# Three chunk splits on VectorE get a fixed place in its queue, in the feed-forward of one decoder layer

## The chip, the core and the metric

The kernel runs on one core of one Trainium2 chip. The metric is device time in microseconds (us) of one execution; lower is better. TensorE multiplies matrices and is called PE in the profile, VectorE is DVE, ScalarE is ACT, GpSimd is POOL, and SyncE, which only issues DMAs here, is SP. PEld is TensorE's weight load.

## What is computed

One layer of a decoder: a gated mix of two attention branches, an attention over 256 memory tokens, a feed-forward and a last normalisation, for 256 tokens of width 1024 in float32. The change lies in the feed-forward:

```python
hn = rmsnorm(h, norm_ffn_g[l])
gu = hn @ w_ffn_in[l]                       # (256, 1024) @ (1024, 2 * 2816)
h = h + (jax.nn.silu(gu[..., :FFN_HIDDEN]) * gu[..., FFN_HIDDEN:]) @ w_ffn_out[l]
...
return rmsnorm(h, final_norm_g)
```

## The kernel before

**Precision.** Every matrix is written as a high and a low part. The high part is a copy in TensorE's reduced float32 format, made by ScalarE; the low part is the source minus the high part, made by VectorE. That pair of operations is called a split. A product of two such matrices is three matmuls: high by high, high by low, low by high.

**Units.** The weights of the feed-forward come in chunks of 1 MB (128 by 2048 float32), one chunk for each unit of work. `FFN_PLAN` (line 90) lists 48 units, and TensorE works through them in this order, which is fixed by hand. The hidden width of 2816 is cut into 11 blocks of 256. Block 0 is made by two units of kind I (2 and 3). Blocks 1 to 10 are taken in pairs, and each pair by seven units of kind P, named P1 to P7: a scheme with seven products in place of eight, in which some products are of sums of token halves (`SS`) with sums of weight chunks, made earlier in DRAM. A unit of kind O multiplies one finished hidden block with its rows of `w_ffn_out` and adds to four accumulators `acc`. The units around the change are: 4 P6, 5 P7, 6 P5, 7 O of block 0, 8 P3, 9 P4 (all of the first pair), 10 P1 and 11 P2 of the second pair, 12 O of block 1, 13 P6, 14 P7, 15 P5, 16 O of block 2. A unit of kind P is 12 matmuls of 128 by 512, a unit of kind O is 24.

**Preparing a unit.** `prep_u(upto)` (line 1172) prepares units up to that number in the program's text: it fetches the chunk by a DMA from SP (line 1157, or 1164 for the chunk of a P2, tile `b`) and calls `halve` (line 1131), which makes the high part in two pieces on ScalarE (line 1146) and, for all but the first units, the low part in one piece on VectorE (line 1151). The fetched chunk lies in one of three buffers `raw`, or in a place that is free at that time (`rawx`). Units whose number divided by 4 leaves 1 put both parts into `px`, from unit 9 on; the others into three buffers `hi` and three `lo`. Behind the split of a P2 unit, GpSimd adds another chunk onto the fetched one by an accumulating DMA (line 1180), and P4 of the same pair uses that sum.

**Gates and turns.** When the products of a block and a token half are done, VectorE puts them together (`whole`, lines 1323 and 1325, tile `fc`), ScalarE takes the silu (`gate`, line 1240, tile `fg`), and VectorE multiplies (lines 1244 and 1246, tile `fu`). For unit 8 the gate reads the bank directly. `turn_hid(o)` (line 1248) then transposes block o on TensorE (line 1253, tile `hidT`) and splits it (lines 309 and 310, tile `hids`), so that a unit of kind O can use it. `TURNS` (line 95) says ahead of which unit a block is turned: block 0 ahead of unit 6, block 1 ahead of unit 10, block 2 ahead of unit 12.

**Order.** TensorE's instructions keep the order of the program's text. Those of the other engines and the DMA issues get an order when the program is built: a planner takes what its model of the chip finds ready, with the earlier one in the text first, and writes each engine's queue. On the chip each of these queues is then worked off in the written order, and an instruction whose operand isn't ready keeps those behind it waiting. Only units 5 and 6 are marked so that their splits keep the text's order.

The main loop (lines 1377 to 1390) runs over units 4 to 45: it prepares a unit some three or four ahead, turns a block where `TURNS` says so, and does the unit's matmuls.

Of the kernel before, what the change touches and what calls it, by code (L numbers as in the profile page):

```python
# [11 lines left out]
F32 = mybir.dt.float32  # L12
# [3 lines left out]
ALU = mybir.AluOpType  # L16
# [128 lines left out]
def build(tc, A, out):  # L145
    nc = tc.nc
    V, SC, G, PE, SY = nc.vector, nc.scalar, nc.gpsimd, nc.tensor, nc.sync
    with ExitStack() as ctx:
# [12 lines left out]
        def big(tag, name, shape=(128, 8, 256), dt=F32):  # L161
            return bp.tile(list(shape), dt, name=name, tag=tag)
# [103 lines left out]
        def by_k(w, k):  # L266
            return tuple(t.rearrange("p (k c) -> p k c", k=k) for t in w)
# [39 lines left out]
        def split(src, hi, lo, scale=None):  # L307
            if scale is None:
                SC.activation(hi, src, AF.Copy)
                V.tensor_tensor(lo, src, hi.bitcast(F32), op=ALU.subtract)  # L310
            else:
                SC.activation(hi, src, AF.Copy, scale=scale)
                V.scalar_tensor_tensor(lo, src, scale, hi.bitcast(F32), op0=ALU.mult, op1=ALU.subtract)
# [742 lines left out]
        def scores(x):  # L1056
            ps = bank("xs", (128, 2, 256))
            for t in range(2):
                a = slice(t * 128, (t + 1) * 128)
                for i in range(2):  # L1060
                    k = 2 * x + i
                    mm3t(ps[:, t], qxh[:, k, a], qxl[:, k, a], kxh[:, k], kxl[:, k], i == 0, i == 1)
            mx, s = small("xmx", [2]), small("xsum", [2])
            p = t2("xp", (128, 2, 256))
            for t in range(2):
                V.tensor_tensor_reduce(out=p[:, t], in0=ps[:, t], in1=mem["rows"], op0=ALU.mult, op1=ALU.max,
                                       scale=1.0, scalar=-3e38, accum_out=mx[:, t:t + 1])
            V.scalar_tensor_tensor(mx, mx, -1.0, one["r16"], op0=ALU.mult, op1=ALU.mult)
            for t in range(2):
                SC.activation(p[:, t], p[:, t], AF.Exp, scale=one["r16"][:, t:t + 1], bias=mx[:, t:t + 1],  # L1070
                              accum_out=s[:, t:t + 1])
            V.reciprocal(s, s)
            for t in range(2):
                V.tensor_scalar(p[:, t], p[:, t], s[:, t:t + 1], None, op0=ALU.mult)
            yield 1
            yield 1
            pT = bank("xT", (128, 2, 256))
            for m in range(2):
                for t in range(2):
                    PE.transpose(pT[:, m, t * 128:(t + 1) * 128], p[:, t, m * 128:(m + 1) * 128], ident)  # L1080
            split(pT, ph[:, x], pl[:, x])

        sg = []
        for c in range(4):
            gemm_f(H1, ev_sum(qxh, qxl, c))
            g = scores(c)
# [44 lines left out]
        def halve(raw, n):  # L1131
            def pin(z):
                if n in PINNED:
                    tc.keep_in_program_order(z)

            tags = PAIRS[n] if n < 6 else PAIRS[n % 4 + 2 if n % 4 == 1 else 0]
            if tags == "px":
                hi, lo = px[:, 0:2048], px[:, 2048:4096]
            elif tags:
                hi, lo = (big(tag, name, (128, 2048), F32R) for tag, name in zip(tags, ("hix", "lox")))  # L1140
            else:
                hi = wh.tile([128, 2048], F32R, name="hi", tag="hi")
                lo = wl.tile([128, 2048], F32R, name="lo", tag="lo")
            for c in range(2):
                a = slice(c * 1024, (c + 1) * 1024)
                pin(SC.activation(hi[:, a], raw[:, a], AF.Copy))  # L1146
            pieces = 2 if n < 2 else 1
            w = 2048 // pieces
            for c in range(pieces):
                a = slice(c * w, (c + 1) * w)  # L1150
                pin(V.tensor_tensor(lo[:, a], raw[:, a], hi[:, a].bitcast(F32), op=ALU.subtract))  # L1151
            return hi, lo

        def fetch(src):
# [6 lines left out]
        def operand(q, name):  # L1161
            if name == "P2" and q != DOUBLES[0]:
                blk[q] = big(next(homes), "b21", (128, 2048))
                tc.keep_in_program_order(SY.dma_start(blk[q], block(q, "21")))
                return blk[q]
            if name == "P4" and q in blk:
                return blk.pop(q)
            return fetch(scr[q][name] if name in scr[q] else block(q, {"P1": "11", "P2": "21", "P3": "22"}[name]))
# [3 lines left out]
        def prep_u(upto):  # L1172
            while made_u[0] <= min(upto, len(units) - 1):
                n = FIRST[made_u[0]] if made_u[0] < len(FIRST) else made_u[0]
                made_u[0] += 1
                u = units[n]
                raw = operand(u[1], u[2]) if u[0] == "P" else fetch(A["w"][where[u]])
                pair[n] = halve(raw, n)
                if u[0] == "P" and u[1] in blk and u[2] == "P2":
                    G.dma_start(raw, scr[u[1]]["P6"], accum_op=ALU.add)  # L1180
# [4 lines left out]
        ssq2 = cp.tile([128, 4], F32, name="ssq2")  # L1185
        v2 = cp.tile([128, 2], F32, name="v2")
        r2 = cp.tile([128, 2], F32, name="r2")
        h2g = {}

        def add_h2(t, c, ps):  # L1190
            d = H[:, t, c * 512:(c + 1) * 512]
# [27 lines left out]
        for t in range(2):  # L1219
            for c in range(2):  # L1220
                ps = mm.tile([128, 512], F32, name="pso", tag="mm")
# [12 lines left out]
        hid, acc, psi, hm = {}, {}, {}, {}  # L1234


        def gate(o, t, sign=1.0):
            ps = psi.pop((o, t))
            g = t2b("fg", (128, 256))
            SC.activation(g, ps[:, 0:256], AF.Silu, scale=sign)  # L1240
            if o not in hm:
                hm[o] = t2("fu", (128, 2, 256))
            if sign < 0:
                V.scalar_tensor_tensor(hm[o][:, t], ps[:, 256:512], sign, g, op0=ALU.mult, op1=ALU.mult)  # L1244
            else:
                V.tensor_tensor(hm[o][:, t], ps[:, 256:512], g, op=ALU.mult)

        def turn_hid(o):
            bk = mm.tile([128, 2, 256], F32, name="hidT", tag="mm")
            u = hm.pop(o)  # L1250
            for t in range(2):
                for j in range(2):
                    PE.transpose(bk[:, j, t * 128:(t + 1) * 128], u[:, t, j * 128:(j + 1) * 128], ident)
            z = o // 2 % 2
            if z not in hids:
                hids[z] = big(("B7", "B14")[z], "hids", (128, 2, 2, 2, 256), F32R)
            hd = hids[z][:, o % 2]
            split(bk, hd[:, 0], hd[:, 1])
            hid[o] = hd

        def out_part(o, w, t, c, home=None, u=0, v=512):
# [58 lines left out]
        def whole(q, t, ps, key):  # L1320
            c = t2("fc")
            if key == "4":
                V.scalar_tensor_tensor(c, ps, -1.0, kept.pop(key), op0=ALU.mult, op1=ALU.subtract)
            else:
                V.tensor_tensor(c, ps, kept.pop(key), op=ALU.add)
            psi[q, t] = c
            gate(q, t)

        def ffn_product(n):
            _, q, name = units[n]  # L1330
            w = by_k(pair[n], 4)
            key = {"P1": "A", "P6": "A", "P5": "A", "P3": "A", "P2": "B", "P7": "F", "P4": "F"}[name]
            first = name in ("P1", "P2", "P7")
            if first:
                bank_of[key] = mm.tile([128, 512], F32, name="pq" + key, tag="mm")
            ps = bank_of[key]
            product(ps, name, w, first)
            if name == "P1":
                keep("1", ps, t2("f1"))
            elif name == "P2":  # L1340
                whole(q + 1, 0, ps, "1")
            elif name == "P6":
                keep("2", ps, gf[:, 1024:1536])
            elif name == "P5":
                keep("4", ps, gf[:, 1536:2048])
                whole(q, 1, bank_of["F"], "4")
            elif name == "P3":
                psi[q, 0] = ps
                gate(q, 0, -1.0)
            elif name == "P4":  # L1350
                whole(q + 1, 1, ps, "2")

        def ffn_out(n):
            w = by_k(pair[n], 2)
# [20 lines left out]
            ffn_in(n, 1)  # L1375
        prep_u(7)
        for n in range(4, len(units) - 2):
            if n != 6:
                prep_u(max(n + 3, min(n + 4, 9)))
            for o in TURNS.get(n, ()):  # L1380
                turn_hid(o)
            prep_u(n + 3)
            u = units[n]
            if u[0] == "I":
                for t in range(2):
                    ffn_in(n, t)
            elif u[0] == "P":
                ffn_product(n)
            else:
                ffn_out(n)  # L1390
# [3 lines left out]
        n = NF // 2 - 1  # L1394
# [38 lines left out]
        with tc.manual_schedule(engines={E.Activation, E.DVE, E.Pool, E.SP}):  # L1433
# [24 lines left out]
            for i in range(2):  # L1458
                a = slice(512 + 256 * i, 768 + 256 * i)
# [46 lines left out]
```

## Time and profile before

| what | value |
|---|---|
| time, median of 3 runs | 612.86 us (612.53 to 612.93) |
| the profiled execution's own time | 612.86 us |
| its span, first to last instruction | 611.1 us |
| TensorE's mean granted clock | 0.998 of full speed |
| busy: TensorE, VectorE, ScalarE, GpSimd | 602.2, 448.9, 373.1, 110.0 us |
| feed-forward and end, in the span | from about 436 us |

A row of a timeline reads: start in us, duration in us, engine, line of the kernel, operation, the tile written and the tiles read, shape and type, and how many instructions were merged into the row; in square brackets, the time for which the engine sat idle before it and what ended that. A busy matmul row of 0.39 us overlaps the next one, as matmuls are pipelined. The chain that ended last follows the work back from the last instruction, each step to what released it.

### The profile page before, as it was taken

The page shows a single profiled execution, that of the slowest core. Times are in us where ns is not written, and L with a number is a line of the kernel's source. Part 1 is how long each engine was busy: PE and PEld are TensorE (multiplying, and loading weights), DVE is VectorE, ACT ScalarE, POOL GpSimd, SP SyncE. Part 2 cuts the span into 40 slices and gives each one's busy share as a digit, 9 for nine tenths or more (in the row PEclk, how much of TensorE's full clock was granted, in tenths as well). Part 3 has the DMA queues.
Part 4 walks back from the last instruction along what each step waited for, and adds up shares of the span by engine and source line. Part 5 has one row for each costly group of instructions (what it writes and reads, how often), then busy time and mean ns, then how long its engine had stood idle before and what let it go on. Part 6 is the DMA issues. An engine that isn't in the chain of part 4 may idle for free.

```text
span 611.1 us, 8304 instructions
## 1 busy us (share of the span) xinstructions
PE 602.2 (99%) x3093; PEld 502.9 (82%) x3093; DVE 448.9 (73%) x702; ACT 373.1 (61%) x603; POOL 110.0 (18%) x137
## 2 busy tenths in 40 slices
PE   8999999999999999999999999999999999999995
PEld 7888888888887887778888888888878888888884
DVE  7598867978756877658866566694896887878953
ACT  7695545333377676736447656684776667677732
POOL 3898100112200431000301403100000000000003
PEclk9999999999999999999999999999999999999999
DMA  8886688747995789957779778863949979796601
GB/s 346 348 305 197 217 252 327 246 139 285 322 257 220 242 260 285 330 203 317 275 216 308 233 280 225 253 215 132 351 158 335 369 267 391 235 383 220 248 2 69
DMA packets 21864, 156.79 MB, mean 257 GB/s; under 512 B 2752, under 2 KB 3392, under 8 KB 5312
## 3 DMA queue, kind: packets, MB, share of 16 engines
q1 hardware_dynamic: 18224, 134.46, 56.7%
q0 software_dynamic: 2880, 20.97, 17.4%
q10 hardware_dynamic: 720, 0.84, 0.4%
q8 instruction: 24, 0.39, 0.3%
q14 instruction: 16, 0.13, 0.1%
HBM read 155.21 MB, written 34.60 MB: 311 GB/s over the span
## 4 chain that ended last, share of the span: by engine, by line
PE 90%; DVE 5%; ACT 2%; issue 1%; POOL 0%; POOLq 0%; DVEq 0%; ACTq 0%
PE pst L262 13%; PE pst L264 13%; PE pst L263 13%; PE pqA L1311 8%; PE psf L283 7%; PE pqF L1311 4%; PE psf L284 4%; PE acc L264 3%; PE acc L263 3%; PE acc L262 3%; PE pqB L1311 2%; PE lp L637 2%; DVE lo L1151 1%; PE psg L538 1%; PE as L826 1%
## 5 line engine op out<-in xcount | busy, mean ns | idle before, releaser
L222 DVE TENSOR_TENSOR lo<-raw,hi 128x1024 fp32r<-128x1024 f32 (+1 forms) x128 | 156.5, 1233 | 56.5 <-ACT hi L221 56.1
L221 ACT ACTIVATE hi<-raw 128x1024 fp32r<-128x1024 f32 (+1 forms) x128 | 129.0, 1028 | 98.5 <-PE pst L264 79.3
L262 PE MATMUL pst<-hi,XX 128*128 128x512 f32 x224 | 90.4, 404 | 0.0
L264 PE MATMUL pst<-hi,XX 128*128 128x512 f32 x224 | 87.4, 390 | 0.0
L263 PE MATMUL pst<-lo,XX 128*128 128x512 f32 x224 | 87.3, 390 | 0.0
L264 PEld LDWEIGHTS pst<-hi,XX 128*128 128x128 f32 x224 | 42.0, 188 | 9.0
L262 PEld LDWEIGHTS pst<-hi,XX 128*128 128x128 f32 x224 | 42.1, 188 | 8.8 <-issue 0.7
L263 PEld LDWEIGHTS pst<-lo,XX 128*128 128x128 f32 x224 | 42.1, 188 | 7.9
L1151 DVE TENSOR_TENSOR lo<-raw,hi 128x2048 fp32r<-128x2048 f32 (+1 forms) x18 | 36.8, 2052 | 10.6 <-ACT hi L1146 10.5
L1146 ACT ACTIVATE hi<-raw 128x1024 fp32r<-128x1024 f32 x32 | 32.0, 1052 | 7.4 <-PE acc L264 5.3
L1151 DVE TENSOR_TENSOR lo<-rawx,hi 128x2048 fp32r<-128x2048 f32 x12 | 27.5, 2288 | 8.1 <-ACT hi L1146 8.1
L1146 ACT ACTIVATE hi<-rawx 128x1024 fp32r<-128x1024 f32 x24 | 24.1, 1051 | 5.9 <-PE acc L264 2.6
L1311 PE MATMUL pqA<-hi,SS 128*128 128x512 f32 x80 | 26.4, 390 | 0.0
L1180 POOL DMA_DIRECT2D b<-t x4 | 3.6, 894 | 124.3 <-DVE fu L1244 124.3
L264 PE MATMUL acc<-hi,hids 128*128 128x512 f32 x62 | 24.3, 392 | 0.7 <-DVE hids L310 0.7
L262 PE MATMUL acc<-hi,hids 128*128 128x512 f32 x62 | 24.4, 393 | 0.0
L263 PE MATMUL acc<-lo,hids 128*128 128x512 f32 x62 | 24.2, 390 | 0.0
L283 PE MATMUL psf<-H,hi 128*128 128x512 f32 x64 | 22.7, 398 | 0.0
L283 PE MATMUL psf<-M,hi 128*128 128x512 f32 x64 | 22.5, 394 | 0.0
L283 PE MATMUL psf<-XX,hi 128*128 128x512 f32 x64 | 22.4, 394 | 0.0
L743 POOL DMA_DIRECT2D t<-w x16 | 13.8, 878 | 46.7 <-DMA t<-w 32.1
L1151 DVE TENSOR_TENSOR lo<-b,hi 128x2048 fp32r<-128x2048 f32 x7 | 16.0, 2292 | 6.2 <-ACT hi L1146 6.2
(418 smaller groups left out, 1511.7 us busy)
## 6 DMA issues: line engine op xcount, KB each, us to landing
raw<-w SPq DMA_DIRECT2D x75, 1024.0 KB, 6.3
t<-w POOLq DMA_DIRECT2D x16, 1024.0 KB, 10.0
raw<-t SPq DMA_DIRECT2D x12, 1024.0 KB, 6.8
rawx<-w SPq DMA_DIRECT2D x10, 1024.0 KB, 7.2
rawx<-t SPq DMA_DIRECT2D x4, 1024.0 KB, 8.9
b<-w SPq DMA_DIRECT2D x4, 1024.0 KB, 9.3
b<-t POOLq DMA_DIRECT2D x4, 1024.0 KB, 8.5
raw<-w SPq DMA_DIRECT2D x4, 512.0 KB, 6.5
```

What stands on the lines that cost most here:

```text
L221: SC.activation(hi[:, a], raw[:, a], AF.Copy)
L222: V.tensor_tensor(lo[:, a], raw[:, a], hi[:, a].bitcast(F32), op=ALU.subtract)
L262: PE.matmul(ps, xh, h, start=first, stop=False)
L263: PE.matmul(ps, xh, l, start=False, stop=False)
L264: PE.matmul(ps, xl, h, start=False, stop=last)
L283: PE.matmul(ps, w[0][:, k, a], X2[:, :, k], start=k == 0, stop=False)
L284: PE.matmul(ps[:, 0], w[1][:, k, a], X2[:, 0, k], start=False, stop=k == 7)
L637: PE.matmul(ps[:, j], KS[:, a0 + j], QQ[:, a0 + j], start=True, stop=True)
L743: tc.keep_in_program_order(G.dma_start(t, block(q, name), accum_op=ALU.add, max_dma_last_dim=8192))
L1146: pin(SC.activation(hi[:, a], raw[:, a], AF.Copy))
L1151: pin(V.tensor_tensor(lo[:, a], raw[:, a], hi[:, a].bitcast(F32), op=ALU.subtract))
L1311: PE.matmul(ps, x[k], z[:, k], start=first and k == 0 and i == 0, stop=k == 3 and i == 2, skip_group_check=not first)
```

## The change

The program gives three low-part splits of `halve` an edge in VectorE's queue: the split of unit 9 is to come behind the low-part split of turn 0, that of unit 11 behind the gate's product of unit 8, and that of unit 13 behind both the gate's product of unit 9 and the low-part split of turn 1. Such an edge, `tc.issue_after(ins)`, is an order within one engine's queue; it adds no instruction and no semaphore. Since the edge can only name an instruction that is in the text already, the preparations move in the text: unit 9 is prepared after turn 0 (before: one unit earlier, ahead of the matmuls of unit 5), unit 11 after the matmuls of unit 8 (before: ahead of them), unit 13 after turn 1 (before: ahead of it). Nothing that is computed changes, and no instruction is added or removed.

```diff
         def split(src, hi, lo, scale=None):
...
-                V.tensor_tensor(lo, src, hi.bitcast(F32), op=ALU.subtract)
+                return V.tensor_tensor(lo, src, hi.bitcast(F32), op=ALU.subtract)
...
             for c in range(pieces):
                 a = slice(c * w, (c + 1) * w)
-                pin(V.tensor_tensor(lo[:, a], raw[:, a], hi[:, a].bitcast(F32), op=ALU.subtract))
+                with ExitStack() as then:
+                    for ins in behind.get(n, ()):
+                        then.enter_context(tc.issue_after(ins))
+                    pin(V.tensor_tensor(lo[:, a], raw[:, a], hi[:, a].bitcast(F32), op=ALU.subtract))
...
-            split(bk, hd[:, 0], hd[:, 1])
+            lo = split(bk, hd[:, 0], hd[:, 1])
+            if o < 2:
+                behind.setdefault(9 + 4 * o, []).append(lo.ins)
...
             elif name == "P3":
                 psi[q, 0] = ps
-                gate(q, 0, -1.0)
+                u = gate(q, 0, -1.0)
+                if n == 8:
+                    behind[11] = [u.ins]
             elif name == "P4":
-                whole(q + 1, 1, ps, "2")
+                u = whole(q + 1, 1, ps, "2")
+                if n == 9:
+                    behind.setdefault(13, []).append(u.ins)
...
         for n in range(4, len(units) - 2):
-            if n != 6:
-                prep_u(max(n + 3, min(n + 4, 9)))
+            if n not in (6, 8, 10):
+                prep_u(max(n + 3, min(n + 4, 8)))
             for o in TURNS.get(n, ()):
                 turn_hid(o)
-            prep_u(n + 3)
+            if n != 8:
+                prep_u(n + 3)
```

`gate` and `whole` now also return the VectorE instruction that writes `fu`.

More of the change, by code (lines that the diff above doesn't have):

```diff
@@ L1187, in build @@
         r2 = cp.tile([128, 2], F32, name="r2")
-        h2g = {}
+        h2g, behind = {}, {}
         def add_h2(t, c, ps):
@@ L1243, in gate @@
             if sign < 0:
-                V.scalar_tensor_tensor(hm[o][:, t], ps[:, 256:512], sign, g, op0=ALU.mult, op1=ALU.mult)
-            else:
-                V.tensor_tensor(hm[o][:, t], ps[:, 256:512], g, op=ALU.mult)
+                return V.scalar_tensor_tensor(hm[o][:, t], ps[:, 256:512], sign, g, op0=ALU.mult, op1=ALU.mult)
+            return V.tensor_tensor(hm[o][:, t], ps[:, 256:512], g, op=ALU.mult)
         def turn_hid(o):
@@ L1326, in whole @@
             psi[q, t] = c
-            gate(q, t)
+            return gate(q, t)
         def ffn_product(n):
```

## The prediction

> **What bounds the kernel now.** I read the page first, then the waits of TensorE (PE) in the feed-forward, then the order of VectorE (DVE) around the one wait found, then how much time every other consumer there has left.
>
> ```profile
> span 611.1 us, 8304 instructions
> PE 602.2 (99%) x3093; PEld 502.9 (82%) x3093; DVE 448.9 (73%) x702; ACT 373.1 (61%) x603; POOL 110.0 (18%) x137
> PE 90%; DVE 5%; ACT 2%; issue 1%; POOL 0%; POOLq 0%; DVEq 0%; ACTq 0%
> ```
>
> PE is busy for 602.2 of 611.1 us and makes 90% of the chain that ended last. A change that moves only VectorE work can win no more than the time for which PE waits for VectorE. The list of PE's waits from 405 us to the end has one row:
>
> ```profile
> PE acc L264 <- DVE hids L310: 0.7, 1, 0.7
> ```
>
> So the whole stage that the change touches holds one wait of PE. The timeline of VectorE shows what stood before that split (lines 307 to 310, called from `turn_hid`), and how the queue goes on:
>
> ```profile
> 453.29 2.29 DVE L1151 TENSOR_TENSOR lo<-rawx,hi 128x2048 fp32r<-128x2048 f32 x1
> 455.49 2.29 DVE L1151 TENSOR_TENSOR px<-raw,px 128x2048 fp32r<-128x2048 f32 x1
> 457.70 0.69 DVE L310 TENSOR_TENSOR hids<-hidT,hids 128x512 fp32r<-128x512 f32 x1
> 458.30 0.69 DVE L1323 SCALAR_TENSOR_TENSOR fc<-pqF,gf 128x512 f32<-128x512 f32 x1
> 463.34 2.29 DVE L1151 TENSOR_TENSOR lo<-rawx,hi 128x2048 fp32r<-128x2048 f32 x1 [3.44 <-ACT hi L1146]
> 465.91 2.29 DVE L1151 TENSOR_TENSOR lo<-b,hi 128x2048 fp32r<-128x2048 f32 x1 [0.28 <-ACT hi L1146]
> 468.12 0.42 DVE L1244 SCALAR_TENSOR_TENSOR fu<-pqA,fg 128x256 f32<-128x256 f32 x1
> 469.22 0.69 DVE L1325 TENSOR_TENSOR fc<-pqF,gf 128x512 f32<-128x512 f32 x1 [0.68 <-PE pqF L1311]
> 469.82 2.28 DVE L1151 TENSOR_TENSOR lo<-rawx,hi 128x2048 fp32r<-128x2048 f32 x1
> 472.02 0.42 DVE L1246 TENSOR_TENSOR fu<-fc,fg 128x256 f32<-128x256 f32 x1
> 472.36 2.29 DVE L1151 TENSOR_TENSOR px<-raw,px 128x2048 fp32r<-128x2048 f32 x1
> 474.56 0.69 DVE L310 TENSOR_TENSOR hids<-hidT,hids 128x512 fp32r<-128x512 f32 x1
> ```
>
> The rows name tiles, not units. Units 9 and 13 are the only ones here that write `px`; 11 is the one read from `b`. The other L1151 rows are then units 8, 10 and 12. The gate of unit 8 is the row of L1244; L1325 and L1246 are `whole` and gate of unit 9; the L310 rows are turns 0 and 1. And ScalarE (ACT), for the same stretch:
>
> ```profile
> 454.58 0.60 ACT L309 ACTIVATE hids<-hidT 128x512 fp32r<-128x512 f32 x1 [1.35 <-PE hidT L1253]
> 463.87 2.01 ACT L1146 ACTIVATE hi<-b 128x1024 fp32r<-128x1024 f32 x2 [0.56 <-DMA b<-w]
> 466.56 0.38 ACT L1240 ACTIVATE fg<-pqA 128x256 f32<-128x256 f32 x1 [0.68 <-PE pqA L1311]
> 466.83 2.00 ACT L1146 ACTIVATE hi<-rawx 128x1024 fp32r<-128x1024 f32 x2
> 471.28 0.57 ACT L309 ACTIVATE hids<-hidT 128x512 fp32r<-128x512 f32 x1
> ```
>
> Turn 0's high part is done at 454.58 + 0.60 = 455.18. Its low part could start when VectorE leaves unit 8's split, at about 455.5; it starts at 457.70, because unit 9's split stands in between. Unit 9 is multiplied long after that, as PE's timeline shows:
>
> ```profile
> 457.14 0.39 PE L262 MATMUL acc<-hi,hids 128*128 128x512 f32 x1
> 458.44 0.50 PE L264 MATMUL acc<-hi,hids 128*128 128x512 f32 x1 [0.68 <-DVE hids L310]
> 463.57 0.39 PE L1311 MATMUL pqA<-hi,SS 128*128 128x512 f32 x1
> 466.30 2.88 PE L1311 MATMUL pqF<-px,H 128*128 128x512 f32 x12
> 469.02 0.60 PE L1253 MATMUL hidT<-cst,fu 128*128 128x128 f32 x4
> 472.45 0.39 PE L1311 MATMUL pqB<-lo,H 128*128 128x512 f32 x1
> 474.95 0.60 PE L1253 MATMUL hidT<-cst,fu 128*128 128x128 f32 x4
> 475.62 0.40 PE L263 MATMUL acc<-lo,hids 128*128 128x512 f32 x1
> 475.85 0.40 PE L264 MATMUL acc<-hi,hids 128*128 128x512 f32 x1
> 480.87 2.88 PE L1311 MATMUL pqA<-px,SS 128*128 128x512 f32 x12
> 489.03 0.39 PE L262 MATMUL acc<-hi,hids 128*128 128x512 f32 x1
> 494.47 2.88 PE L1311 MATMUL pqA<-px,SS 128*128 128x512 f32 x12
> ```
>
> **The size of the wait.** Unit 7, with the wait, runs from 457.14 to the start of unit 8 at 463.57: 6.43 us. Unit 16, the same 24 matmuls without a wait, runs from 489.03 to 494.47: 5.44 us. The wait costs 6.43 − 5.44 = 0.99 us, not the 0.68 us of the wait's own entry, since the pipeline also refills. I take 0.99; the lower bound is 0.68.
>
> **The change, part by part.** No instruction is added or dropped. An edge in VectorE's own queue needs no semaphore; what changes is order.
>
> *First edge (unit 9's split behind turn 0's).* Turn 0's split moves to about 455.5 to 456.2. Unit 9's 12 matmuls span 466.30 to 469.02, 0.23 each; turn 0's matmul would be due two spacings after 457.14, at 457.6, so 1.4 us are left over. Gain 0.99. Unit 9's split moves to about 456.1 to 458.4, due at 466.5 − 0.99 = 465.5: 7 us left. `whole` of unit 6 (458.30) stays where it was.
>
> *What is late next.* PE now arrives 0.99 us earlier everywhere, while splits paced by a DMA do not. Unit 8's product `fu` ends at 468.12 + 0.42 = 468.54; turn 1 needs it at 469.02 − 0.99 = 468.03. Left in its place it would be 0.51 us late. Turn 1's split ends at 474.56 + 0.69 = 475.25; its matmul is due at 475.85 − 0.99 = 474.86: 0.39 late. The first edge alone would give about half of its gain back.
>
> *Second edge (unit 11's split behind unit 8's `fu`).* PE frees unit 8's bank 0.99 earlier, at about 465.5, but ACT is on unit 11's high part until 463.87 + 2.01 = 465.88. The gate then takes 465.9 to 466.3 and `fu` 466.3 to 466.7, 1.3 us ahead of 468.03. The new wait is VectorE's: it idles from 465.6 to 466.3, and unit 11's split stands behind, at 466.7 to 469.0 instead of ending at 468.2. It is due at 472.45 − 0.99 = 471.46: 2.4 us left. Behind it come `whole` of unit 9 (469.0 to 469.7) and unit 12's split (to 471.9, due at 475.62 − 0.99 = 474.63). The idle 0.7 us replaces the 0.68 us idle that VectorE now has before 469.22, so the queue is no later after it.
>
> *Third edges (unit 13's split behind unit 9's `fu` and turn 1's split).* `fu` falls at 472.0 to 472.4, against turn 2 at 474.95 − 0.99 = 473.96: 1.5 left. Turn 1's split follows to 473.1, against 474.86: 1.8 left. Unit 13's goes to 473.1 to 475.4, against 480.87 + 0.23 − 0.99 = 480.1: 4.7 left. Should unit 12's split pass `whole` of unit 9, `fu` ends 0.5 us later and 1.0 is left.
>
> *Queues that are passed.* A weight buffer is refilled only after its split. The rows:
>
> ```profile
> 436.66 0.33 SPq L1157 DMA_DIRECT2D raw<-t  x1
> 457.81 0.33 SPq L1157 DMA_DIRECT2D raw<-t  x1
> 475.19 2.01 ACT L1146 ACTIVATE hi<-raw 128x1024 fp32r<-128x1024 f32 x2 [0.28 <-ACT hi L1146]
> 468.85 0.91 POOL L1180 DMA_DIRECT2D b<-t  x1 [34.61 <-DVE fu L1244]
> 494.72 2.01 ACT L1146 ACTIVATE hi<-b 128x1024 fp32r<-128x1024 f32 x2 [2.69 <-issue]
> ```
>
> Unit 9's own fetch goes out at 436.66, 19 us before its split. The change traces it after turn 0, but its buffer came free before, so I expect it to stay. The refill behind unit 9's split (457.81, unit 15) goes out 0.6 us later for a first use at 475.19: hidden. POOL's accumulation onto `b` at 468.85 goes out about 0.8 us later; what it makes is read at 494.72: hidden. If either cover were gone, the price would be those 0.6 or 0.8 us.
>
> At that accumulation a rule speaks against the change:
>
> ```profile
> 499.30 2.28 DVE L1151 TENSOR_TENSOR px<-raw,px 128x2048 fp32r<-128x2048 f32 x1
> 499.46 0.88 POOL L1180 DMA_DIRECT2D b<-t  x1 [29.70 <-DVE fu L1244]
> ```
>
> These two overlap, and neither is longer than elsewhere (2.28 and 0.88, against 2.29 and 0.91). The Trainium skill, "SBUF — State Buffer", section "Who interferes with whom", says that VectorE and GpSimd share ports under an exclusive lock, and that a VectorE operation with two SBUF inputs contends with GpSimd's reads, the later one blocking fully. After the change the accumulation falls beside unit 12's split; by the rule that split could be held for 0.9 us, the margin of 1.0 to 1.5 us at turn 2 would shrink to 0.1 to 0.6, and the sum would still be the same. The overlap above shows no such hold, so I give it nothing.
>
> **The sum.** 611.1 − 0.99 = 610.1 us of span. The profiled run took 612.86 us, 1.76 us outside its span, and equals the median; 612.86 − 0.99 = **611.9 us**. After 458.44 PE has no other wait up to the end, and VectorE, ACT and the loads there are mostly released by PE, so I expect the lead of 0.99 us to be carried to the end whole.
>
> **The rivals.**
>
> *The wait moves (partial gain).* One consumer is late after all: `fu` of unit 8 because ACT takes unit 12's high part (2.00 us) before the gate. Then `fu` ends near 466.3 + 2.0 + 0.4 = 468.7, 0.65 us late, and the time is 612.86 − 0.99 + 0.65 = 612.5. For it: margins of 1.0 to 1.8 us are smaller than one split. Against: ACT takes the gate before that high part now (466.56, 466.83).
>
> *Slower: another split goes into the place that is freed.* VectorE keeps its queue's order (turn 0's split, ready at 455.18, waited its turn until 457.70), and unit 11's split leaves a hole before `fu`. If unit 12's split is put there, it waits for its high part, which ends at 466.3 + 2.0 = 468.3; the split ends at 470.5, `fu` at 470.9, and turn 1, due at 468.03, starts near 471.0. That costs 2.97 us, less the 0.99 won: 612.86 + 1.98 = 614.8. It decides when the planned order has the split of unit 12 ahead of L1244. For it: the order already is not the program's. Against: on ACT the gate comes first, so `fu` is ready 1.6 us before that split.
>
> *The change does not do what it says.* Turn 0's split stays behind some other operation, or a loss elsewhere of the same size appears: 612.9. Nothing that could be ready at 455.5 is in sight.
>
> **How the numbers follow.** Forecast (611.6 to 612.1) 0.65; partial 0.13; no effect 0.05; slower 0.13; more gain than the one wait holds 0.04. The range of 611.5 to 613.4 takes in the forecast, the lower bound of the wait (612.2), the partial case and no effect; it leaves out the slower rival. A measurement of this kernel can tell about 0.2%, 1.23 us, from no change; the forecast of 0.99 us (0.16%) lies inside that. Faster than 611.63: 0.10, the edge of the forecast. Slower than 614.09: 0.13. Within: 0.77.
>
> **What would show it.** Right: no wait of PE at L264 near 458; unit 7 takes 5.44 us; L310 starts near 455.5, before the `px` row; L1244 starts near 466.3, before the `b` row; the second L310 comes before the second `px` row; PE's last matmul ends 0.99 us earlier. Wrong: a new row in PE's waits, above all hidT on `fu` or `acc` on `hids`; or unit 12's split ahead of L1244.

## The result, and the profile after

The changed kernel takes 611.09 us (median of 9 runs, 610.86 to 611.81) against 612.80 us for the kernel before in the same runs: a ratio of 0.9978 (95% interval 0.9969 to 0.9987). By the medians it is faster by 1.71 us, 0.28%. The forecast was 611.9 us with a range down to 611.5, so the direction was right and the size too small; the time lies outside the range.

Of the page of the changed kernel, the span, the busy times and the chain by engine:

```profile
span 609.1 us, 8302 instructions
PE 600.9 (99%) x3093; PEld 502.1 (82%) x3093; DVE 449.1 (74%) x702; ACT 373.1 (61%) x603; POOL 110.5 (18%) x137
PE 97%; DVE 1%; issue 1%; ACT 0%; POOL 0%; POOLq 0%; DVEq 0%
```

VectorE has as many instructions as before (702; the two fewer in the total are waits on semaphores in the queues); its share of the chain fell from 5% to 1%. The list of TensorE's waits from 400 us on has lost the wait of `acc` on `hids`. What is left is a small one in the attention over the memory tokens, which the change does not touch:

```profile
PE xT L1080 <- DVE xp L1074: 0.2, 1, 0.2
```

VectorE's timeline around the turns (the lines of the file moved: the chunk splits are L1154 now, the gate's products L1247 and L1248, `whole` L1329):

```profile
452.30 2.28 DVE L1154 TENSOR_TENSOR lo<-rawx,hi 128x2048 fp32r<-128x2048 f32 x1
454.50 0.68 DVE L310 TENSOR_TENSOR hids<-hidT,hids 128x512 fp32r<-128x512 f32 x1
455.11 2.28 DVE L1154 TENSOR_TENSOR px<-raw,px 128x2048 fp32r<-128x2048 f32 x1
...
465.37 0.42 DVE L1247 SCALAR_TENSOR_TENSOR fu<-pqA,fg 128x256 f32<-128x256 f32 x1 [0.52 <-ACT fg L1243]
465.71 2.28 DVE L1154 TENSOR_TENSOR lo<-b,hi 128x2048 fp32r<-128x2048 f32 x1
467.91 0.68 DVE L1329 TENSOR_TENSOR fc<-pqF,gf 128x512 f32<-128x512 f32 x1
468.91 2.29 DVE L1154 TENSOR_TENSOR lo<-rawx,hi 128x2048 fp32r<-128x2048 f32 x1 [0.32 <-ACT hi L1146]
471.12 0.42 DVE L1248 TENSOR_TENSOR fu<-fc,fg 128x256 f32<-128x256 f32 x1
471.46 0.68 DVE L310 TENSOR_TENSOR hids<-hidT,hids 128x512 fp32r<-128x512 f32 x1
472.06 2.28 DVE L1154 TENSOR_TENSOR px<-raw,px 128x2048 fp32r<-128x2048 f32 x1
```

The three moves are there as written: turn 0's split (454.50) ahead of unit 9's `px`, unit 8's `fu` (465.37) ahead of unit 11's `b`, unit 9's `fu` and turn 1's split (471.12, 471.46) ahead of unit 13's `px`. Two rows of TensorE mark the stage in the kernel before, the second matmul of unit 7 and the last matmul of the kernel:

```profile
457.37 0.39 PE L263 MATMUL acc<-lo,hids 128*128 128x512 f32 x1
...
604.39 0.28 PE L264 MATMUL end<-hi,hids 128*128 128x256 f32 x1
```

And in the changed kernel the same two, with the start of unit 7, of unit 8 and the two consumers that the prediction watched, between them:

```profile
456.16 0.39 PE L262 MATMUL acc<-hi,hids 128*128 128x512 f32 x1
456.38 0.39 PE L263 MATMUL acc<-lo,hids 128*128 128x512 f32 x1
...
461.60 0.39 PE L1315 MATMUL pqA<-hi,SS 128*128 128x512 f32 x1
467.04 0.60 PE L1255 MATMUL hidT<-cst,fu 128*128 128x128 f32 x4
473.87 0.40 PE L264 MATMUL acc<-hi,hids 128*128 128x512 f32 x1
...
602.41 0.28 PE L264 MATMUL end<-hi,hids 128*128 128x256 f32 x1
```

Unit 7 takes 461.60 − 456.16 = 5.44 us, and from its second matmul to the last one it is 602.41 − 456.38 = 146.03 us against 604.39 − 457.37 = 147.02. So the stage gave 0.99 us. But the two profiled runs are 612.86 − 610.88 = 1.98 us apart, and unit 7 is already 0.99 us earlier in the second (456.38 against 457.37). That part comes from the first ten microseconds. The first real matmuls of the kernel, eight of line 538, in the kernel before and then in the changed one:

```profile
5.17 3.14 PE L538 MATMUL psg<-hi,XX 128*128 128x512 f32 x8
```

```profile
5.06 2.23 PE L538 MATMUL psg<-hi,XX 128*128 128x512 f32 x8
```

The same eight matmuls end at 8.31 and at 7.29 us. In the trace of the kernel before the first of them start 0.43 us apart, then 0.23: TensorE's clock opened 7.45 us after the span's start there, and 5.05 us after it in the other. The change alters no instruction in that place.

### The profile page after: what moved, and what is told of

Same layout as the page of the kernel before. It is cut to its first block, busy times and chain, and to the rows that moved or that the text cites. A ratio compares the mean times of both kernels' runs of the same rounds, so it can differ in the third digit from the quotient of the medians.

```text
span 609.1 us, 8302 instructions
## 1 busy us (share of the span) xinstructions
PE 600.9 (99%) x3093; PEld 502.1 (82%) x3093; DVE 449.1 (74%) x702; ACT 373.1 (61%) x603; POOL 110.5 (18%) x137
## 4 chain that ended last, share of the span: by engine, by line
PE 97%; DVE 1%; issue 1%; ACT 0%; POOL 0%; POOLq 0%; DVEq 0%
PE pst L262 13%; PE pst L264 13%; PE pst L263 13%; PE pqA L1315 9%; PE psf L283 7%; PE pqF L1315 4%; PE psf L284 4%; PE acc L264 3%; PE acc L263 3%; PE acc L262 3%; PE pqB L1315 2%; PE lp L637 2%; PE psg L538 1%; PE pso L264 1%; PE pso L263 1%; PE pso L262 1%
## 5 line engine op out<-in xcount | busy, mean ns | idle before, releaser
L1154 DVE TENSOR_TENSOR lo<-raw,hi 128x2048 fp32r<-128x2048 f32 (+1 forms) x18 | 36.8, 2051 | 10.6 <-ACT hi L1146 10.5
L1154 DVE TENSOR_TENSOR lo<-rawx,hi 128x2048 fp32r<-128x2048 f32 x12 | 27.5, 2288 | 7.5 <-ACT hi L1146 7.5
L1154 DVE TENSOR_TENSOR px<-raw,px 128x2048 fp32r<-128x2048 f32 x8 | 18.3, 2284 | 2.2 <-ACT px L1146 2.2
```

## The experiments

"Stage" in the table is the time from unit 7's second matmul to the last matmul of the kernel, in the profile of that run; the waits are TensorE's after 400 us, without the one of 0.2 us shown above. Ratios are to the kernel before on the same chip, with a 95% interval.

| run | what | ratio | median us | stage us | waits of TensorE |
|---|---|---|---|---|---|
| before | | | 612.80 | 147.02 | acc on hids 0.7 |
| before_again | the same | 1.0000 (0.9983 to 1.0018) | 612.80 | 147.03 | acc on hids 0.7 |
| before_third | the same | 0.9994 (0.9982 to 1.0005) | 612.64 | 147.80 | acc on hids 0.7, hidT on fu 0.6 |
| edges_2_3 | unit 9 as before | 1.0004 (0.9986 to 1.0023) | 612.61 | 147.03 | acc on hids 0.7 |
| first_edge | only unit 9 moved | 0.9998 (0.9981 to 1.0015) | 612.13 | 146.66 | acc on hids 0.2 |
| edges_1_2 | unit 13 as before | 0.9999 (0.9984 to 1.0014) | 612.25 | 146.68 | acc on hids 0.4 |
| text_only | text moved, no edge | 0.9991 (0.9978 to 1.0004) | 612.41 | 146.65 | hidT on fu 0.4 |
| one_edge | text moved, unit 11's edge | 0.9995 (0.9982 to 1.0008) | 612.62 | 146.03 | none |
| after | the change | 0.9978 (0.9969 to 0.9987) | 611.09 | 146.03 | none |
| after_again | the same | 0.9973 (0.9959 to 0.9988) | 611.45 | 146.03 | none |
| after_third | the same | 0.9970 (0.9959 to 0.9980) | 611.41 | 146.03 | none |
| after_fourth | the same | 0.9994 (0.9973 to 1.0015) | 611.54 | 146.03 | none |

**The two kernels again.** No edit.

> The kernel before, unchanged, timed against itself. Theory A (the change is worth only TensorE's wait of 0.99 us; the rest of the measured 1.7 us is the moment at which TensorE's clock opens at the start, which differs between executions of one and the same kernel): single times scatter by up to some 1.5 us, in step with how long the first eight matmuls of line 538 take (2.2 us with the clock open, 3.1 us and more with it late), and the ratio is 1.000 within about 0.15%. Theory B (the changed program itself opens the clock earlier): every execution of this kernel has the late start, first eight matmuls about 3.1 us, and times within 0.4 us of 612.7.

> The changed kernel, unchanged, timed again. Theory A: ratio between 0.9970 and 0.9995 with a scatter of up to 1.5 us; its span less what the late clock costs is 0.99 us under that of the kernel before, and the wait at the first unit of kind O is gone. Theory B: ratio 0.997 to 0.998 again and the early clock in the profile.

The start of `before_again`:

```profile
5.04 2.65 PE L538 MATMUL psg<-hi,XX 128*128 128x512 f32 x8
```

The kernel before has an early start too: here the eight matmuls take 2.65 us, and this profiled run took 612.18 us, 0.68 less than the one of 612.86, with the same stage (147.03). From the end of the eight matmuls, 7.69 against 8.31 us, comes 0.62 of the 0.68. Its single times run from 612.18 to 615.07 us, eight of the twelve up to 613.03. So theory B as it was worded, a late start in every execution of the kernel before, falls. That the change always brings an early start falls too: in `after_late256` below, which has the change, the eight matmuls take 3.07 us. A weaker lean is not excluded, as `after_again` itself met both expectations (ratio 0.9973, eight matmuls in 2.32 us). And theory A had the medians 0.99 us apart, and they are 1.35 us apart here (612.80 − 611.45), in `after_third` 1.47 (612.88 − 611.41). Some of the gain was still missing.

**One part at a time.** The core of the edits; `edges_1_2` and `edges_2_3` also leave out the edge whose unit they put back:

```diff
 first_edge:
-            if o < 2:
+            if o < 1:
...
-                if n == 8:
-                    behind[11] = [u.ins]
...
-            if n not in (6, 8, 10):
+            if n != 6:
...
 text_only:
-                    for ins in behind.get(n, ()):
+                    for ins in ():
...
 edges_1_2:
-            if n not in (6, 8, 10):
+            if n not in (6, 8):
...
 edges_2_3:
-                prep_u(max(n + 3, min(n + 4, 8)))
+                prep_u(max(n + 3, min(n + 4, 9)))
```

> Only the first edge: unit 9's split behind turn 0's; units 11 and 13 as in the kernel before. By the prediction the wait at 458 goes, 0.99 us are won there, and then turn 1 waits 0.51 us for the product of unit 8's gate and perhaps up to 0.39 us for the split of turn 1: a net gain of 0.1 to 0.5 us. Rival: the later consumers are not late, and this alone gives the whole 0.99 us.

> The preparations stand in the text as in the changed kernel, but no edge is given. In VectorE's queue as planned, units 9 and 13 come behind the turns by their place in the text alone, unit 11 stays ahead of the product of unit 8's gate. Prediction's reasons: a wait of about 0.5 us at turn 1 for that product, none at turn 1's split: a net gain of about 0.5 us. Rival: the same 0.99 us as the changed kernel, which would make the edges needless.

> First and second edge, unit 13 as in the kernel before. Prediction's reasons: no wait at 458 and none at turn 1 for the gate's product, but turn 1's split stands behind unit 13's and comes 0.4 to 0.5 us late: one wait of acc on hids near 474, and the way from unit 7 to the last matmul 0.5 us longer than in the changed kernel (146.5 us against 146.03). Rival (the third edges are needless): 146.0 us and no wait.

> Second and third edges, unit 9's split ahead of turn 0's as in the kernel before. Prediction's reasons: the wait of 0.68 us at 458 stays and nothing else waits, so from unit 7 to the last matmul it takes 147.0 us as before, and the time is that of the kernel before. Rival (the edges win by themselves, by shortening something further on): under 146.8 us.

TensorE's waits in the four, in the order `first_edge`, `text_only`, `edges_1_2`, `edges_2_3`:

```profile
PE acc L264 <- DVE hids L310: 0.2, 1, 0.2
```

```profile
PE hidT L1255 <- DVE fu L1247: 0.4, 1, 0.4
```

```profile
PE acc L264 <- DVE hids L310: 0.4, 1, 0.4
```

```profile
PE acc L264 <- DVE hids L310: 0.7, 1, 0.7
```

Each consumer that the prediction called late is late when its part alone is left out. Without the second edge turn 1 waits for `fu` (stage 146.65, 0.62 over the changed kernel). Without the third, `acc` waits for turn 1's split (146.68, 0.65 over). With the first edge alone, the stage keeps only 147.02 − 146.66 = 0.36 of the 0.99; the prediction had 0.1 to 0.5. Turn 1 itself is hardly late there (11.01 us behind unit 7's start, against 10.88 in the changed kernel), because unit 11's load took 7.8 us in that execution and not 8.2 as in the profile of before; turn 1's split costs the rest. Without the first edge nothing is won (147.03). The ratios of these four cannot tell 0.4 us from nothing; the stage in the profile can.

**Which edge does the work.** In `text_only` VectorE's queue has two of the three moves without any edge, since unit 9's and unit 13's preparations stand behind the turns in the text. So one edge should do:

```diff
-                    for ins in behind.get(n, ()):
+                    for ins in behind.get(n, ()) if n == 11 else ():
```

> The text order of the changed kernel with one edge only, that of unit 11. In the queues as planned every engine has the order of the changed kernel, so both theories expect its time; a wait in the profile, or another time than the changed kernel's by over 0.3 us in the mean of the bulk, would mean that an edge costs or brings something by itself.

The stage is that of the changed kernel (146.03). The times are not: the median is 612.62, though in the traces of `one_edge` and `after_third` every engine works off the same instructions in the same order. In its profile TensorE waits elsewhere, ahead of the feed-forward:

```profile
PE aT L850 <- DVE ap L842: 0.2, 1, 0.2
```

Around that matmul (190 us) this execution loses 0.6 us against `after_third`. What came late is a load again: ScalarE waits for a weight chunk, and VectorE's split of that chunk stands ahead of `ap`. In `after_third` the same operation starts 0.85 us earlier:

```profile
184.45 1.06 ACT L221 ACTIVATE hi<-raw 128x1024 fp32r<-128x1024 f32 x1 [2.90 <-DMA raw<-w]
```

```profile
183.60 1.06 ACT L221 ACTIVATE hi<-raw 128x1024 fp32r<-128x1024 f32 x1 [2.17 <-PE as L826]
```

That chunk landed 17.8 us after its fetch, later than in any other profile without a held start (12.5 to 17.2). Why the median lies 1.2 us above those of `after_third` and `after_fourth`, taken on the same chip, stays open.

**More of the same two.** No edit.

> The kernel before once more, to see how its single times are spread. Theory A (change worth 0.99 us, the start differs by itself): the bulk between 612.0 and 613.3 us as until now, with its mean at 612.6; where the profile's clock opens tells its place in that range, and from unit 7 to the last matmul it takes 147.03 us. Theory B (before has another slow place that comes and goes, beside the start): in some profile the stretch from 100 matmuls on to unit 7 is longer than in the others.

> The changed kernel once more. Theory A: the bulk spread as that of the kernel before and about 1.0 us lower, mean near 611.6; 146.03 us from unit 7 to the last matmul. Theory B (worth more than the wait): mean near 611.1.

> The same again, for the spread. Theory A: mean of the bulk near 611.6; theory B: near 611.1. Single times of 613.8 us and more, which the kernel before has in some of its executions, should come here as often (one in six or seven) if they have nothing to do with the change.

`before_third` brought what was missing. Its waits of TensorE, then ScalarE on unit 11's high part, SP's fetch of that chunk, VectorE and TensorE at turn 1:

```profile
PE acc L264 <- DVE hids L310: 0.7, 1, 0.7
PE hidT L1253 <- DVE fu L1244: 0.6, 1, 0.6
```

```profile
464.76 2.01 ACT L1146 ACTIVATE hi<-b 128x1024 fp32r<-128x1024 f32 x2 [0.56 <-DMA b<-w]
```

```profile
455.41 0.33 SPq L1164 DMA_DIRECT2D b<-w  x1
```

```profile
469.02 0.42 DVE L1244 SCALAR_TENSOR_TENSOR fu<-pqA,fg 128x256 f32<-128x256 f32 x1
```

```profile
469.49 0.66 PE L1253 MATMUL hidT<-cst,fu 128*128 128x128 f32 x4 [0.57 <-DVE fu L1244]
```

From the fetch to the first operation on `b` it takes 464.76 − 455.41 = 9.35 us here; in the profile of before it was 8.2 (455.64 to 463.87), and 7.4 to 8.4 in the eleven profiles without a held start or an added copy, this one left out. Unit 11's split came that much later, unit 8's `fu` stood behind it, and turn 1 waited: the stage takes 147.80 us, 0.78 more. This is theory B of these expectations in another guise: the kernel before has a second wait that comes and goes with a load, though it lies in the stage and not ahead of it. The other two runs decide little: the mean of `after_third` is 611.36 us and that of nine of the times of `after_fourth` 611.47, between the 611.6 of theory A and the 611.1 of theory B. `after_fourth` also shows that single times above 614 us, three of its twelve, are not tied to the kernel before; they widen its interval.

**A late load on purpose.** SP issues a copy within DRAM between the fetches of units 10 and 11, into a scratch tensor that nothing reads:

```diff
-                tc.keep_in_program_order(SY.dma_start(blk[q], block(q, "21")))
+                with ExitStack() as then:
+                    if q == 3:
+                        then.enter_context(tc.issue_after(sent[0].ins))
+                        e = SY.dma_start(extra[:, 0:512], block(9, "21")[:, 0:512])
+                        then.enter_context(tc.issue_after(e.ins))
+                    tc.keep_in_program_order(SY.dma_start(blk[q], block(q, "21")))
```

`sent[0]` is the fetch before; with 512 KB the width is 1024.

> The kernel before with a copy of 256 KB within DRAM issued by SP between the fetches of units 10 and 11, so that unit 11's chunk lands later by d, about 0.7 to 1.4 us. Theory C (unit 11's split, paced by its load, stands ahead of unit 8's product, and the margin of 0.48 us is used up by a late load): a second wait, of hidT on fu, and 147.03 + d - 0.4 us from unit 7 to the last matmul, so 147.3 to 148.0. Theory A (only the one wait): 147.03.

> The changed kernel with the same copy. Theory C: no wait of hidT, 146.03 us from unit 7 to the last matmul, since unit 8's product no longer stands behind that split. Rival: it is late here too, because unit 8's gate still stands behind unit 11's high part on ScalarE: 146.2 and more.

> The same with 512 KB, d about 1.3 to 2.7 us. Theory C: the second wait grows by as much as the landing is later than with 256 KB; 148 to 149.5 us from unit 7 to the last matmul. Theory A: 147.03.

> The same for the changed kernel. Theory C: 146.0 to 146.3 us, as the margin at turn 1 is 1.3 us by the prediction and 2.4 us at unit 11 itself; beyond those it waits too.

| run | ratio | median us | stage us | waits of TensorE |
|---|---|---|---|---|
| before_late256 | 1.0015 (0.9987 to 1.0044) | 613.91 | 147.87 | acc on hids 0.7, hidT on fu 0.7 |
| before_late512 | 1.0024 (1.0000 to 1.0049) | 614.18 | 147.93 | acc on hids 0.7, hidT on fu 0.7 |
| after_late256 | 0.9987 (0.9969 to 1.0006) | 612.03 | 146.03 | none |
| after_late512 | 1.0002 (0.9981 to 1.0022) | 612.83 | 146.03 | none |

SP in the profile of before, then SP and VectorE in `before_late256`:

```profile
454.13 0.33 SPq L1157 DMA_DIRECT2D rawx<-w  x1
455.64 0.33 SPq L1164 DMA_DIRECT2D b<-w  x1
```

```profile
455.11 0.33 SPq L1160 DMA_DIRECT2D rawx<-w  x1
455.50 0.50 SPq L1170 DMA_DIRECT2D extra<-w  x1
456.63 0.34 SPq L1172 DMA_DIRECT2D b<-w  x1
```

```profile
468.12 2.29 DVE L1151 TENSOR_TENSOR lo<-b,hi 128x2048 fp32r<-128x2048 f32 x1 [1.57 <-ACT hi L1146]
470.33 0.42 DVE L1252 SCALAR_TENSOR_TENSOR fu<-pqA,fg 128x256 f32<-128x256 f32 x1
```

And VectorE in `after_late256`:

```profile
466.87 0.42 DVE L1255 SCALAR_TENSOR_TENSOR fu<-pqA,fg 128x256 f32<-128x256 f32 x1 [0.42 <-ACT fg L1251]
467.82 2.29 DVE L1154 TENSOR_TENSOR lo<-b,hi 128x2048 fp32r<-128x2048 f32 x1 [0.53 <-ACT hi L1146]
```

The late load costs the kernel before 0.85 and 0.91 us in the stage and the changed one nothing: theory C. The medians are 1.88 us apart with 256 KB (613.91 and 612.03) and 1.35 us with 512 KB (614.18 and 612.83), where the stages are 1.84 and 1.90 us apart; the two medians of the changed kernel differ by 0.80 us with the same stage. All four profiles also take some 0.5 us longer behind the last matmul than those without the copy, which no run explains.

One expectation missed: 512 KB delay no more than 256 KB. The fetch itself does not go out later. It follows unit 10's by 456.63 − 455.11 = 1.52 us with the copy between them and by 455.64 − 454.13 = 1.51 us without, since in both SP waits for a split on VectorE before it (0.6 us with the copy, 1.1 without). What is later is the landing: from the fetch to the first operation on `b` it takes 9.45 and 9.49 us in the kernel before and 9.97 and 9.43 in the changed one, with 256 and 512 KB, against 8.23 in the profile of before. Why twice the bytes make no difference is open.

A limit of this test: the order on ScalarE is not that of the kernels without the copy. In the changed kernel unit 8's gate now stands between the two halves of unit 11's high part, so that queue helped there, and in the kernel before a piece of unit 13 stands ahead of unit 12's high part; VectorE's order was that of before or of the change.

**A start held back (failed).** To take the start's scatter out, the first real matmul was made to wait for five clearings of a tile by GpSimd, behind 40 warming matmuls.

```diff
-WARM = 15
+WARM = 40
...
+        slow = big("B12", "slow", (128, 2048))
+        for _ in range(5):
+            G.memset(slow, 0.0)
+        PE.matmul(warm[:, 0:1], slow[:, 0:128], ones, start=True, stop=True)
```

> The kernel before with its first real matmul held back: 40 warming matmuls in place of 15, and behind them one matmul that reads a tile which GpSimd clears five times, so that TensorE's clock should be open before real work starts. Nothing of the result changes. Theory A (the scatter of about 1.2 us among the executions of one kernel is the moment at which the clock opens): the bulk of the single times lies within 0.5 us; the start is later by 2 to 6 us, and the time longer by about as much. Rival (the scatter comes from elsewhere, such as the loads): still over 1 us.

> The changed kernel with the same held-back start. Theory A: its times too lie within 0.5 us, and their median is 0.99 us (0.8 to 1.2) below that of the kernel before with the held-back start. Theory B (the changed program wins 1.7 us): 1.5 us or more below.

It told nothing about the question. The times spread more, 618.87 to 625.25 for the kernel before (median 624.19, ratio 1.0161, 1.0129 to 1.0194) and 619.33 to 623.62 for the changed one (median 622.47, ratio 1.0145, 1.0124 to 1.0167), and ScalarE's and VectorE's planned order early in the kernel changed with it. GpSimd's timeline in `before_open` shows why the spread grew:

```profile
0.72 7.51 POOL L362 MEMSET slow<- 128x2048 f32 x4 [0.29 <-POOLq L1501]
10.01 0.19 POOL L398 CAST posf<-gv 128x2 f32<-128x2 int32 x1 [1.78 <-DMA gv<-gv]
10.14 1.80 POOL L362 MEMSET slow<- 128x2048 f32 x1
```

The planner put another operation, which waits for a load, ahead of the fifth clearing, so the gate hung on that load.

## Why the prediction was wrong

**What bounds the kernel, and the size of the wait: right.** The wait cost 0.99 us, as worked out from units 7 and 16 (147.02 − 146.03), and not the 0.68 us of its own entry.

**The three edges, and what is late next: right.** Turn 0's split followed unit 8's at once. Left in their old places, unit 8's `fu` and turn 1's split cost the stage 0.62 and 0.65 us (they were expected to be 0.51 and 0.39 us late); in the changed kernel neither waits. Unit 9's and unit 13's edges turned out to be what the text's order gives anyway; only unit 11's edge is needed beside it.

**The queues that are passed: right.** No load or accumulation is waited for. The rule on shared ports from the Trainium skill, "SBUF — State Buffer", section "Who interferes with whom", which spoke against the change, shows in no row here. The same section says that a `tensor_tensor` did not stall a DMA in its own probe, so this split need not be a case for it. GpSimd's issue stands beside unit 12's split, 468.91 for 2.29 us, and is as long as before:

```profile
468.82 0.91 POOL L1183 DMA_DIRECT2D b<-t  x1 [35.57 <-issue]
```

**The sum: this step failed.** It took 0.99 us from the time of one profiled execution, which "equals the median", as if that execution stood for all and only the stage could differ. The stage did give 0.99 us, but the medians moved by 1.71 us, and by 1.34 to 1.47 us in the three repeats (612.80 − 611.45, 612.88 − 611.41, 612.88 − 611.54). So 0.35 to 0.72 us of the difference have no term in the sum. Where they come from stays open; what the runs show is that executions differ in three places. Take from an execution's time its stage and the start of TensorE's 101st matmul, some 25 us in: what is left is 440.16 to 440.24 us in eleven of the twelve profiles without an added copy or a held start, and 440.8 in the twelfth, `one_edge`.

First, the kernel's start differs by itself. The profiled run of before had the clock open late (3.14 us for the eight matmuls), the profiled run after early (2.23); this gave 0.99 of the 1.98 us between them. The 101st matmul starts at 24.99 to 25.63 us in the three profiles of before and at 24.65 to 25.25 in the four of the changed kernel: the ranges overlap, and so few profiles cannot tell whether the change has a part in it. The Trainium skill, "TensorE: Matmul & The Clock Gate", section "Part 1: The HAM clock gate", says that the hardware watches TensorE's activity in a free-running window of about 3.4 us, so that the moment at which the clock opens varies from run to run; it measured about 0.5 us to either side. The openings seen here, at 5.05, 6.21 and 7.45 us, vary too, by 2.40 us in all; no run here shows the window itself.

Second, the margin of 0.48 us between unit 8's `fu` (468.54) and turn 1 (469.02) in the kernel before was read only for what happens once TensorE comes earlier. That the load ahead of it varies by a microsecond was not weighed. In an execution where it lands late, the kernel before pays 0.78 us more; the changed one paid nothing in the test with the copy, so the change is worth 1.77 us there and 0.99 elsewhere. One of the three profiled executions of the unchanged kernel before had that wait, but the landing was that late in only one of all twelve profiles. How often it comes in the executions that were only timed is not known, and at one in twelve it would hardly move a median.

Third, a late load near 190 us cost `one_edge` 0.6 us. That run also shows how far medians go: one order of instructions gave 611.41, 611.54 and 612.62 us on one chip. By such a spread the exact miss is partly chance: of the four medians of the changed kernel, 611.09 is the lowest, two more lie just under the range (611.41, 611.45) and one inside it (611.54).

**The rivals and the range.** None of the rivals came. The range had no room for more than 0.99 us except 0.4 for nothing named; a rival "the kernel before has waits that this execution doesn't show" was missing, and its price, up to the span of unit 11's load, could have been bounded by the landing times (8.1 to 11.8 us for the four fetches into `b` in the profile of before).

## What to carry to other kernels

A wait is worth the stretch around it with the wait less the same stretch without it, and removing it makes the consumers next in line late; here each of them had to be moved too, or two thirds of the gain were lost again. In a queue that is worked off in order, an operation that waits for a load should not stand ahead of one that the bounding engine needs soon, even where the one profile at hand shows a margin: the margin has to cover the spread of the load. Before a forecast is measured against a median, see how far the start and the loads alone move the time of one and the same kernel; a stretch between two marks in the trace told 0.4 us here where the medians did not.

## What was not expected of the hardware

- The same program, with the same stage times, spread by more than 1 us from execution to execution. In the profiles of the two kernels the first eight matmuls took 2.23 to 3.14 us, while from TensorE's 101st matmul to unit 7 it took 431.48 to 431.53 us in every profile without a held start except `one_edge` (432.09).
- One and the same 1 MB fetch, that of unit 11, issued 1.5 us ahead of unit 7, was first read 7.4 to 8.4 us later in eleven profiles and 9.35 us later in one; behind a copy within DRAM of 256 or of 512 KB it was 9.4 to 10.0 us.
- While GpSimd cleared the tile in `before_open`, VectorE's cast of 128x256 took 1.46 us; in the kernel before it takes 0.29. "SBUF — State Buffer" of the Trainium skill, section "Who interferes with whom", says that VectorE's copies and casts can contend with GpSimd for shared ports, where the later operation waits until the earlier one is done. This row agrees: the cast ends at 2.67 us, just behind the first of the four clearings, which began at 0.72 us and take 7.51 us together.

```profile
1.21 1.46 DVE L356 CAST still<-zero 128x256 fp32r<-128x256 f32 x1
```
